# Inverting the softmax sums of a head pair as 16 columns by way of DRAM, in place of a 128x512 reciprocal

## The chip, the cores and the metric

The kernel runs on one core of a Trainium2 chip. The metric is device microseconds of one execution: the median of three runs is 2515.03 us (2510.77 to 2517.75). One more execution was profiled; it took 2517.77 us, and its trace has a span of 2516.0 us.

## The reference, cut to what matters

The program is two transformer blocks over 1024 tokens of width 1024, in float32. Its first block has two attention layers. Layer 0 mixes eight heads of global attention, eight of windowed attention and four memory heads; layer 1 mixes sixteen heads of neighbourhood attention and four memory heads. The part that the change touches is the division in the softmax of the global and the neighbourhood heads:

```
s = jnp.einsum('bqkgd,bskd->bkgqs', qblk, k).astype(jnp.float32) * scale
p = jax.nn.softmax(s, axis=-1).astype(v.dtype)
return jnp.einsum('bkgqs,bskd->bqkgd', p, v)
...
y = jnp.concatenate([ya, yb, ym], axis=-1) * jax.nn.silu(gate)
x = x + y @ w_out_even[e]
```

A sum belongs to a query and a head, so a pair of heads has 2 x 1024 different sums. The second block (a pooling mixer and a convolutional feed-forward part) isn't touched.

## The kernel before, in words

Every matmul operand is split into a high and a low part, and a product is three matmuls (`mm3`, L251 to L255; a weight's low part is `wlo`, made in `sub`, L142). Two streams of work are interleaved. The *attention stream* runs the heads two at a time (`pipe`): `glob_main` for four pairs of layer 0, `win_main` for four windowed pairs, and `nbr_main` for eight pairs of layer 1. The *fill stream* runs the projections (`dense`), which load weights into three buffers `wraw`. `weave` mixes both streams by a planned cost for each step; `ahead` gives the attention stream a higher priority; the framework's scheduler then fixes one order of instructions for each engine ahead of the run. Each engine works through its order strictly, and an instruction that waits holds up what is behind it. All DMAs are issued by SyncE (SP) in one such order (`dma`, L162).

The global and the neighbourhood pairs use `wide`. Their queries lie along 1024 columns in two halves g of 512. O is one buffer of 128 x 1024 (two heads of 64 rows; `bufs` is 1, so the next pair writes it only when this one's is stored). For each head s and key tile, ScalarE computes p, GpSimd (POOL) adds p to `acc[s, g]` (L586), and TensorE adds to o. When a half is complete, `close` copies half of o on ScalarE (`oe`, L605) and VectorE adds the two parts into O (L606). After the second head's half, TensorE sums `acc` over its partitions by matmuls with a matrix of twos: d is a PSUM tile of 128 x 512 in which rows 0 to 63 all hold one head's sums and rows 64 to 127 the other's. VectorE inverts all of d (L618), and POOL multiplies O by the result R (L619). d lies in the one PSUM buffer `r`, which the row-maximum transposes of `max_row` (L461) use too. At the pair's end `finish_pair` loads the gate sg, `back` multiplies O by it on VectorE (L622), and O goes to DRAM (`y<-O`); the last pair of each layer is split into hh and hl instead. `oe`, sg and R share two buffers (tag `oe`); the sums `acc` have four (tag `acc`).

The memory heads (`mem_main`) have a 128x512 reciprocal of their own (L734), which stays.

Of the kernel before, what the change touches and what calls it, by code (L numbers as in the profile page):

```python
# [8 lines left out]
F32 = mybir.dt.float32  # L9
F32R = mybir.dt.float32r  # L10
AF = mybir.ActivationFunctionType
ALU = mybir.AluOpType
# [3 lines left out]
S = 1024  # L16
# [120 lines left out]
def raw(ap):  # L137
    return ap.bitcast(F32) if ap.dtype == F32R else ap


def sub(out_eng, out, a, b):
    out_eng.tensor_tensor(out=out, in0=a, in1=b, op=ALU.subtract)  # L142


class Build:
# [411 lines left out]
    def wide(self, O, U, V, tiles, perm=False):  # L557


        nc = self.nc  # L560
        mm = nc.tensor.matmul
        parts = [[(g, max(a, 512 * g), min(b, 512 * g + 512)) for g in range(2) if max(a, 512 * g) < min(b, 512 * g + 512)] for _, a, b in tiles]
        touch = {g: [i for i, ps in enumerate(parts) if g in [p[0] for p in ps]] for g in range(2)}
        acc, bank = {}, {}

        def sums(s, g):
            acc[s, g] = t = self.po.tile([128, 512], F32, tag="acc", name="acc", bufs=self.accb)
            return t

        def dest(s, i):  # L570

            g, a, b = parts[i][0]
            if (s, g) not in acc:
                return sums(s, g)
            return self.pp.tile([128, b - a], F32, tag="p", name="p", bufs=3)

        def take(s, i, p):

            a = tiles[i][1]
            for g, x0, x1 in parts[i]:  # L580
                if (s, g) not in acc:
                    nc.gpsimd.memset(sums(s, g), 0.0)
                t = acc[s, g]
                if t is not p:
                    t = t[:, x0 - 512 * g:x1 - 512 * g]
                    nc.gpsimd.tensor_tensor(out=t, in0=t, in1=p[:, x0 - a:x1 - a], op=ALU.add)  # L586

        def pv(s, i, P):
            j, a, b = tiles[i]
            for g, x0, x1 in parts[i]:  # L590
                new = (s, g) not in bank
                if new:
                    bank[s, g] = self.op.tile([128, 512], F32, tag="od"[g], name="o")
                o = bank[s, g][:, x0 - 512 * g:x1 - 512 * g]
                x = slice(x0 - a, x1 - a)
                mm(o, V[s][:, j, 2:130], P[0][:, x], start=new, stop=False, skip_group_check=True)
                mm(o[0:64], V[s][:, j, 2:66], P[1][:, x], start=False, stop=i == touch[g][-1], skip_group_check=True)  # L597
                if i == touch[g][-1]:
                    close(s, g)

        def close(s, g):

            o = bank[s, g]
            e = self.po.tile([64, 512], F32, tag="oe", name="oe", bufs=2)
            nc.scalar.copy(e, o[64:128])  # L605
            nc.vector.tensor_tensor(out=self.halfo(O[64 * s:64 * s + 64], g, perm), in0=self.seq(o[0:64], perm), in1=self.seq(e, perm), op=ALU.add)  # L606
            if s == 0:
                return
            d = self.rq.tile([128, 512], F32, tag="r", name="d")
            for i in range(2):  # L610
                h = self.pp.tile([128, 512], F32R, tag="ph", name="ah")
                nc.scalar.copy(h, acc[i, g])
                l = self.pp.tile([128, 512], F32R, tag="pl", name="al")
                sub(nc.gpsimd, l, acc[i, g], raw(h))
                mm(d, self.sel[i], h, start=i == 0, stop=False)
                mm(d, self.sel[i], l, start=False, stop=i == 1)
            R = self.po.tile([128, 512], F32, tag="oe", name="R", bufs=2)
            nc.vector.reciprocal(R, d)  # L618
            nc.gpsimd.tensor_tensor(out=self.halfo(O, g, perm), in0=self.halfo(O, g, perm), in1=self.seq(R, perm), op=ALU.mult)  # L619

        def back(g, sg):
            nc.vector.tensor_tensor(out=self.halfo(O, g, perm), in0=self.halfo(O, g, perm), in1=self.seq(sg, perm), op=ALU.mult)  # L622
        return dest, take, pv, back

    def narrow(self, O, U, V, tiles, groups, sink):
# [28 lines left out]
        def close(s, g, ts):  # L654
# [5 lines left out]
            nc.vector.tensor_tensor(out=e[:, :, 0], in0=e[:, :, 0], in1=sink[s][:, q], op=ALU.add)  # L660
            R = self.small.tile([128, 8], F32, tag="R", name="R")
            nc.vector.reciprocal(R[:, 0:n], e[:, :, 0])
            nc.gpsimd.tensor_tensor(out=T[:, q, s], in0=e[:, :, 2:66], in1=e[:, :, 66:130], op=ALU.add)
            nc.gpsimd.tensor_tensor(out=T[:, q, s], in0=T[:, q, s], in1=R[:, 0:n].unsqueeze(2).to_broadcast([128, n, 64]), op=ALU.mult)

# [992 lines left out]
```

## Time and profile before

| What | us |
|---|---|
| median of three runs | 2515.03 (2510.77 to 2517.75) |
| profiled execution | 2517.77 |
| its span | 2516.0 |
| TensorE (PE) busy | 2397.2, 95% |
| VectorE (DVE) busy | 1809.1, 72% |
| ScalarE (ACT) busy | 1071.7, 43% |
| GpSimd (POOL) busy | 989.7, 39% |
| DMA queue, share of 16 engines | 41.0% |

The global pairs run from about 190 to 560 us of the span and the neighbourhood pairs from about 960 to 1500. A row of the waits names the engine and what it waited for, then the total us, the number of times and the longest one. A busy PE is not PE at its peak, so its granted clock stands beside it. The line numbers are those of the kernel before.

### The profile page before, as it was taken

To read this page: it belongs to the slowest core of one execution; us is meant where nothing else is said; L and a number is where in the kernel's file an instruction comes from. 1 tells how busy PE (TensorE), PEld (TensorE's weight loads), DVE (VectorE), ACT (ScalarE), POOL (GpSimd) and SP (SyncE) were. 2 spreads that over 40 slices of the span, in tenths; PEclk is the share of its full clock that TensorE was granted. 3 is DMA by queue.
4 is the path that set the end of the run, shared out by engine and by line. 5 is a ranking of instruction groups with operands and counts; after the bars stand their busy time and mean duration, and the time that the engine had idled before them with its cause. 6 is when DMAs were issued, how large, how long until landed. Compare 5 with 4: busy or idle time off the path is not lost. (4 is left out here: it accounts for less than half of the span.)

```text
span 2516.0 us, 33273 instructions
## 1 busy us (share of the span) xinstructions
PE 2397.2 (95%) x11320; PEld 1962.2 (78%) x11320; DVE 1809.1 (72%) x2897; ACT 1071.7 (43%) x1873; POOL 989.7 (39%) x833
## 2 busy tenths in 40 slices
PE   7999999999999999999999999998789999999999
PEld 6967777777878788888888877776668888888887
DVE  6778877787787557767888789798967464655554
ACT  5526555554442535444343553444544132323231
POOL 3128886873331226656575762575700000000000
PEclk9999999999899999999999999997979999999999
DMA  6752342344456567766675564321213111111112
GB/s 204 214 135 71 114 109 93 93 128 118 128 186 214 183 190 188 192 191 171 196 204 171 164 238 159 124 82 51 69 45 97 51 49 49 46 51 47 50 47 88
DMA packets 234241, 314.37 MB, mean 125 GB/s; under 512 B 101879, under 2 KB 120823, under 8 KB 234072
## 3 DMA queue, kind: packets, MB, share of 16 engines
q1 hardware_dynamic: 234072, 312.26, 41.0%
q8 instruction: 89, 1.46, 0.2%
q14 instruction: 80, 0.66, 0.1%
HBM read 225.02 MB, written 87.03 MB: 124 GB/s over the span
## 5 line engine op out<-in xcount | busy, mean ns | idle before, releaser
L254 PE MATMUL ps<-hl,whi 128*128 128x512 f32 x1888 | 753.0, 399 | 13.3 <-DVE hl L396 7.8
L251 PE MATMUL ps<-hh,whi 128*128 128x512 f32 x1888 | 749.8, 400 | 15.5 <-ACT hh L395 8.2
L255 PE MATMUL ps<-hh,wlo 128*128 128x512 f32 x1888 | 752.6, 399 | 9.0 <-DVE wlo L142 8.8
L242 ACT CAST whi<-wraw 128x512 fp32r<-128x512 f32 (+1 forms) x416 | 250.7, 606 | 494.9 <-PE ps L254 409.5
L251 PEld LDWEIGHTS ps<-hh,whi 128*128 128x128 f32 x1888 | 363.2, 193 | 92.9 <-ACT hh L395 8.2
L254 PEld LDWEIGHTS ps<-hl,whi 128*128 128x128 f32 x1888 | 363.4, 192 | 92.5 <-DVE hl L396 9.9
L255 PEld LDWEIGHTS ps<-hh,wlo 128*128 128x128 f32 x1888 | 362.8, 192 | 86.1 <-DVE wlo L142 10.8
L586 POOL TENSOR_TENSOR acc<-acc,p 128x512 f32<-128x512 f32 (+2 forms) x272 | 320.0, 1183 | 237.8 <-ACT p L449 186.0
L142 DVE TENSOR_TENSOR wlo<-wraw,whi 128x512 fp32r<-128x512 f32 (+1 forms) x404 | 330.1, 821 | 61.9 <-ACT whi L242 54.3
L142 POOL TENSOR_TENSOR pl<-p,ph 128x512 fp32r<-128x512 f32 (+2 forms) x208 | 259.7, 1251 | 189.4 <-ACT ph L451 163.8
L451 ACT CAST ph<-p 128x512 fp32r<-128x512 f32 (+2 forms) x336 | 181.8, 551 | 40.7 <-PE o L649 10.4
L449 ACT ACTIVATE p<-p 128x256 f32<-128x256 f32 (+2 forms) x192 | 97.7, 515 | 151.0 <-DVE p L1236 94.7
L1480 DVE TENSOR_TENSOR xacc<-ps,xacc 128x512 f32<-128x512 f32 x96 | 66.2, 691 | 131.4 <-PE ps L255 131.0
L1452 DVE TENSOR_TENSOR hz<-ps,rbc 128x512 f32<-128x512 f32 x88 | 60.5, 690 | 116.4 <-PE ps L255 114.2
L142 DVE TENSOR_TENSOR pl<-p,ph 128x512 fp32r<-128x512 f32 (+2 forms) x128 | 115.2, 900 | 39.7 <-ACT ph L451 32.9
L254 PE MATMUL ps<-al,whi 128*128 128x512 f32 x352 | 139.1, 396 | 0.0
L255 PE MATMUL ps<-ah,wlo 128*128 128x512 f32 x352 | 138.8, 396 | 0.0
L251 PE MATMUL ps<-ah,whi 128*128 128x512 f32 x352 | 138.5, 396 | 0.0
L449 ACT ACTIVATE p<-s 128x512 f32<-128x512 f32 x144 | 84.6, 597 | 119.6 <-PE s L538 69.6
L1456 ACT ACTIVATE cv<-hz,vecs 128x512 f32<-128x512 f32 x88 | 71.5, 815 | 130.6 <-DVE hz L1452 125.0
L597 PE MATMUL o<-pl,V 128*64 128x384 f32 (+2 forms) x288 | 94.5, 347 | 3.2 <-DVE pl L142 2.4
L1236 DVE TENSOR_TENSOR p<-s,MB 128x384 f32<-128x384 f32 (+2 forms) x128 | 68.5, 548 | 39.8 <-POOL pl L142 22.5
(268 smaller groups left out, 4563.3 us busy)
## 6 DMA issues: line engine op xcount, KB each, us to landing
wraw<-in_w SPq DMA_DIRECT2D x116, 256.0 KB
wraw<-in_wfi SPq DMA_DIRECT2D x112, 256.0 KB
wraw<-in_wo SPq DMA_DIRECT2D x72, 256.0 KB
g<-evf SPq DMA_DIRECT2D x48, 256.0 KB
wraw<-in_wfo SPq DMA_DIRECT2D x40, 256.0 KB
sg<-g SPq DMA_DIRECT2D x32, 256.0 KB
y<-O SPq DMA_DIRECT2D x14, 512.0 KB
hl<-y SPq DMA_DIRECT2D x14, 512.0 KB
```

Of the source, the lines that this page charges most:

```text
L142: out_eng.tensor_tensor(out=out, in0=a, in1=b, op=ALU.subtract)
L242: nc.scalar.copy(hi, raw[:, q:q + e])
L251: i = mm(ps, wh, h, start=first, stop=False, skip_group_check=True)
L254: mm(ps, wh, l, start=False, stop=False, skip_group_check=True)
L255: mm(ps, wl, h, start=False, stop=last, skip_group_check=True)
L449: nc.scalar.activation(p, s, AF.Exp)
L451: nc.scalar.copy(ph, p)
L586: nc.gpsimd.tensor_tensor(out=t, in0=t, in1=p[:, x0 - a:x1 - a], op=ALU.add)
L597: mm(o[0:64], V[s][:, j, 2:66], P[1][:, x], start=False, stop=i == touch[g][-1], skip_group_check=True)
L1236: nc.vector.tensor_tensor(out=p, in0=ps, in1=MB[:, s, o:o + b - a], op=ALU.add)
L1456: nc.scalar.activation(t, z[:, 2:514], AF.Identity, scale=self.v("cw2", j), bias=self.v("cb", j))
L1480: nc.vector.tensor_tensor(out=x, in0=ps, in1=x, op=ALU.add)
```

## The change

The whole-tile reciprocal and the multiplication directly behind it go. Each half of d is copied by ScalarE as rows 0 to 64, and rows 0 and 64, one for each head, are written to a DRAM tile `dd` of 2 x 1024. After the second half `invert` loads `dd` as 128 partitions x 16 columns, inverts that on VectorE, writes it to a second DRAM tile `dr`, and loads R of both halves by four DMAs that repeat a row over 64 partitions. R now takes buffers of the tag `acc`. POOL's multiplication of O by R moves into `back`, in front of the multiplication by the gate.

```diff
@@ wide @@
         acc, bank = {}, {}
+        dd, dr = [self.dram(n, [2, S], F32) for n in ("dd", "dr")]
+        R = []
...
                 mm(d, self.sel[i], h, start=i == 0, stop=False)
                 mm(d, self.sel[i], l, start=False, stop=i == 1)
-            R = self.po.tile([128, 512], F32, tag="oe", name="R", bufs=2)
-            nc.vector.reciprocal(R, d)
-            nc.gpsimd.tensor_tensor(out=self.halfo(O, g, perm), in0=self.halfo(O, g, perm), in1=self.seq(R, perm), op=ALU.mult)
+            e = self.po.tile([65, 512], F32, tag="oe", name="de", bufs=2)
+            nc.scalar.copy(e, d[0:65])
+            for i in range(2):
+                self.dma(out=dd[i, 512 * g:512 * g + 512], in_=e[64 * i:64 * i + 1])
+            if g == 1:
+                invert()
+
+        def invert():
+
+            c = self.small.tile([128, 16], F32, tag="dc", name="dc")
+            self.dma(out=c, in_=dd.rearrange("h (a b) -> (h a) b", b=16))
+            r = self.small.tile([128, 16], F32, tag="dr", name="dr")
+            nc.vector.reciprocal(r, c)
+            self.dma(out=dr.rearrange("h (a b) -> (h a) b", b=16), in_=r)
+            for g in range(2):
+                R.append(self.po.tile([128, 512], F32, tag="acc", name="R", bufs=self.accb))
+                for i in range(2):
+                    self.dma(out=R[g][64 * i:64 * i + 64], in_=dr[i:i + 1, 512 * g:512 * g + 512].to_broadcast([64, 512]))
 
         def back(g, sg):
+            nc.gpsimd.tensor_tensor(out=self.halfo(O, g, perm), in0=self.halfo(O, g, perm), in1=self.seq(R[g], perm), op=ALU.mult)
             nc.vector.tensor_tensor(out=self.halfo(O, g, perm), in0=self.halfo(O, g, perm), in1=self.seq(sg, perm), op=ALU.mult)
```

## Rows read from the trace of the kernel before

**Rows 1.** Windows: start:end, length, busy us of PE, PEld, DVE, ACT, POOL, PEclk, DMA share, GB/s

```profile
190.00:560.00 370.00, 353.39 (x1544) 273.11 (x1542) 296.77 (x395) 213.08 (x376) 299.75 (x208) 0.98 0.33 101
960.00:1500.00 540.00, 529.04 (x2766) 449.44 (x2765) 419.20 (x694) 244.11 (x475) 337.22 (x324) 0.99 0.65 188
374.00:383.00 9.00, 5.36 (x14) 2.38 (x13) 9.00 (x12) 1.20 (x3) 5.54 (x5) 0.73 0.21 73
1146.00:1154.00 8.00, 5.37 (x18) 3.54 (x17) 8.00 (x18) 1.33 (x3) 1.52 (x1) 0.72 0.59 165
```

**Rows 2.** Groups by line and shape: count, busy us, mean ns, idle before

```profile
L618 DVE RECIPROCAL R<-d 128x512 f32<-128x512 f32 x24 | 80.4, 3350 | 1.4 <-PE d L616 1.3
L619 POOL TENSOR_TENSOR O<-O,R 128x512 f32<-128x512 f32 x24 | 39.7, 1652 | 53.3 <-DVE R L618 51.8 <-DVE negm L1213 1.5
L622 DVE TENSOR_TENSOR O<-O,sg 128x512 f32<-128x512 f32 x24 | 28.1, 1170 | 5.9 <-DMA sg<-g 5.9
L605 ACT COPY oe<-o 64x512 f32<-64x512 f32 x48 | 27.8, 580 | 11.9 <-PE o L597 11.3
...
L359 DVE RECIPROCAL r<-rs 128x16 f32<-128x16 f32 x5 | 1.2, 246 | 1.4 <-ACT rs L357 1.4
```

**Rows 3.** PE's waits in 374:383, 469:473, 1012:1016 and 1147:1152

```profile
PE s L461 <- DVE R L618: 1.4, 1, 1.4
PE o L597 <- DVE pl L142: 1.1, 1, 1.1
PE s L846 <- DVE mcg L847: 0.9, 1, 0.9
...
PE s L461 <- DVE R L618: 1.2, 1, 1.2
PE o L597 <- DVE pl L142: 0.9, 1, 0.9
...
PE ps L251 <- DVE evl L1285: 1.2, 1, 1.2
...
PE ps L255 <- DVE wlo L142: 1.7, 1, 1.7
PE s L461 <- DVE R L618: 0.7, 1, 0.7
```

**Rows 4.** VectorE in order of time: start us, us, line, operation, tiles

```profile
1006.98 3.36 DVE L618 RECIPROCAL R<-d 128x512 f32<-128x512 f32 x1
1010.26 0.39 DVE L1285 SCALAR_TENSOR_TENSOR evl<-ps,rc,evh 128x256 fp32r<-128x256 f32 x1
...
282.73 3.34 DVE L618 RECIPROCAL R<-d 128x512 f32<-128x512 f32 x1
...
299.71 0.67 DVE L606 TENSOR_TENSOR O<-o,oe 64x512 f32<-64x512 f32 x1
...
1435.00 3.35 DVE L618 RECIPROCAL R<-d 128x512 f32<-128x512 f32 x1
...
1449.83 1.06 DVE L606 TENSOR_TENSOR O<-o,oe 64x512 f32<-64x512 f32 x1
```

**Rows 5.** SP's DMA issues in order of time

```profile
1168.20 0.38 SPq L162 DMA_DIRECT2D qc4h<-evh  x1
1169.20 0.33 SPq L162 DMA_DIRECT2D qc4l<-evl  x1
1171.50 1.15 SPq L162 DMA_DIRECT2D U<-qc4h  x2
...
1446.09 0.32 SPq L162 DMA_DIRECT2D y<-O  x1
```

**Rows 6.** Waits of SP and POOL over the span: total us, times, longest

```profile
SPq L162 <- DVE wlo L142: 752.7, 274, 16.1
...
SPq L162 <- DMA x<-xr: 27.4, 10, 4.1
...
POOL O L619 <- DVE R L618: 51.8, 12, 10.6
```

## The prediction, made before the changed kernel was run

> **What bounds the kernel now.** I read the windows by stage first, then the groups by line, then PE's waits, then the order of time on VectorE and SP around a few reciprocals. The windows show that TensorE is the engine that sets the time where the change acts: it is busy 353.4 of 370 us while the global pairs run and 529.0 of 540 us while the neighbourhood pairs do [rows 1]. The reader should see that VectorE's 80.4 us of reciprocals [rows 2] aren't 80 us of the span. What can be had is PE's idle time there, (370 - 353.4) + (540 - 529.0) = 27.6 us, and what a lower clock costs behind a pause. PE's waits show which part of that follows a reciprocal. Eight waits lie in short stretches directly behind four of the 24: three times `max_row`'s matmul waits until R has been read out of the one PSUM buffer `r`, and five times PE waits for something that VectorE had queued behind a reciprocal [rows 3]; one of these is the split of the V projection, which starts at 1010.26, as the 3.36 us reciprocal of 1006.98 ends [rows 4]. Behind two of the four the granted clock has a mean of 0.73 and 0.72, so part of the stretch ran at 1.2 in place of 2.4 GHz [rows 1].
>
> **What goes.** 24 reciprocals of 3.35 us leave VectorE [rows 2]. On the path they are worth what PE waits for them: 1.4 + 1.1 + 0.9 + 1.2 + 0.9 + 1.2 + 1.7 + 0.7 = 9.1 us [rows 3]. The clock adds at most (1 - 0.73) x 9 + (1 - 0.72) x 8 = 4.6 us [rows 1]. Together that is 13.7 us, or 13.7 / 80.4 = 0.17 us of span for each us that VectorE stands in the way; I use this rate below. What is late next in those places is the ScalarE copy of d (0.6 us in place of 3.35), so `r` comes free at least 2.7 us sooner than it does now, more than the longest of the three waits for it (1.4).
>
> **What is added beside other work.** 24 copies of 65 x 512 on ScalarE: the nearest row is the 64 x 512 copy out of PSUM at 0.58 us [rows 2], so 13.9 us. ScalarE is busy 213 of 370 and 244 of 540 us [rows 1], which hides them; if that cover failed everywhere they would cost 13.9 us. Twelve reciprocals of 128 x 16 at 0.25 us [rows 2] are 3 us of VectorE, at the rate 0.5 us; I leave them inside the rounding. The multiplications of O by R are the same 24 at 1.65 us, moved. SP gets ten more DMAs a pair (four writes of `dd`, one load, one write of `dr`, four broadcasts); at the 0.33 to 0.58 us of an issue [rows 5] (the two issues of U take 1.15) that is 3 to 6 us a pair. SP has 752.7 us in which it only waits for a weight buffer [rows 6]; these hide it.
>
> **What is added in series.** Four DMAs now depend on each other: `dd` out, `dd` in, `dr` out, R in. The trace of before has no transfer of 64 bytes a partition and no such chain. The nearest rows are a store and the load of the same tile: the store of qc4h is issued at 1168.20 and its load could be issued at 1171.50, 3.3 us later [rows 5]. On the other side SP stood 27.4 / 10 = 2.7 us, on average, for the store of x1 before it loaded that again [rows 6]. These transfers are 256 KB and the new ones 2 to 128 KB, so a hop may be below 2.7 as well; one that shares the queue with weights, as in the second stage at 188 GB/s [rows 1], may be above 3.3. I take 3.0, between the two rows. R then comes 0.6 (copy) + 4 x 3.0 + 0.25 + 1.0 (three issues behind a first one) = 13.8 us after the point at which the last reciprocal of a pair starts now, and it came 3.35 us after it: 10.5 us later.
>
> Sentences that the sum can do without: the Trainium skill, page "DMA: Bandwidth & Descriptors", section "Anatomy of one DMA — SWDGE (gpsimd) path", gives a small transfer about 2.0 us of fixed cost, nearly all of it the receipt of the write; it measured that on GpSimd's path, and these DMAs are SP's. The rows are above it (2.7 and 3.3), with larger transfers in them. As an estimate by the page, R would come after 0.6 + 8.0 + 0.25 + 1.0 = 9.9 us; the O term below would then be 1.1 in place of 3.7 us, and the sum 2504.5.
>
> **Who waits for R.** First POOL: the multiplication stands in POOL's order, with next pair's `acc` additions and half of its `pl` behind it. POOL stands for R already, 51.8 us in 12 places [rows 6], and no row of PE's waits in the four stretches names POOL [rows 3]. The bounds are 0 and 12 x 10.5 = 126 us of standing, at the rate 0 to 21 us. I take a tenth, 12.6 us or 2.1 us of span, because the order is fixed by a plan that knows of the DMAs, and the standing of today costs nothing visible.
>
> Second, O, which has one buffer. From the old start of the last reciprocal to O's release is now 13.8 + 1.65 + 1.65 (POOL, two halves) + 1.17 (gate, VectorE) + 3.7 (the store: issued at 1446.09, the next write of O follows without idling at 1449.83) = 22.0 us [rows 2, 4, 5]. The next pair's first write of O comes 299.71 - 282.73 = 17.0 us after that start in the first of the ten places where another such pair follows, and 1449.83 - 1435.00 = 14.8 in the last [rows 4]; of the other eight, read in the same way, two are at 15.7 and 18.8 and six at 22 or more. So four writes are late, by 5.0, 6.3, 3.2 and 7.2 = 21.7 us. If VectorE stands for all of that, it costs 21.7 x 0.17 = 3.7 us; 0 if the plan puts other work first, and about 10 if hops are 4.5 us and six of the ten are late. I take 3.7. R in the `acc` buffers meets the next pair's second head only, half a pair later, about 25 us with pairs 60 to 90 us apart; I cost it at nothing.
>
> **The sum.** -13.7 + 3.7 + 2.1 = -7.9 us. The profiled execution takes 2517.8 us, 2.7 above the median of 2515.0; it would become 2509.9, and the median **2507**. About 0.3% (7.5 us) is what a measurement of this kernel can tell from no change, so this stands at that edge.
>
> **The rivals.**
> - *More comes free* (0.12). VectorE is busy 297 of 370 us in the first stage [rows 1]; with 27 us less there, waits go that don't lie behind a reciprocal. At most all 27.6 us of idle time go: 2487; in the middle 2497. Against it: in the second stage PE has only 11 us to give.
> - *Nothing comes of it* (0.18). The fixed order of every engine is planned anew, so other waits of 1 to 2 us open where the eight close, and POOL's and O's terms use up the rest: 2513, within 4.
> - *The chain gets stuck in SP's order* (0.27), and the kernel is slower. SP issues in order and stands 752.7 / 274 = 2.7 us on average before a weight load, 16.1 at the longest [rows 6]. If such a load is ahead of each of the four hops, R is later by another 10.8 us a pair, and POOL stands all of it at the multiplication: 12 x 10.8 = 130 us, at the rate 22 us. The sum is -13.7 + 3.7 + 22 = +12: 2527. It decides from (13.7 - 3.7) / 0.17 = 59 us of POOL's standing, 5 us a pair. For it: an order that waits is SP's normal state. Against it: most of those waits end where the plan expected them, and POOL's standing has not reached PE so far.
>
> The forecast has 0.43, of which 0.31 is faster by over 0.3% and 0.12 within it; its own range is 2500 to 2513. With the rivals: **faster** 0.31 + 0.12 = 0.43; **same** 0.12 + 0.18 = 0.30; **slower** 0.27. The range that should hold the time 8 times in 10 is 2492 to 2529: it takes in the upper part of the first rival's span and the slower rival's 2527.
>
> **What would show it.** Right: no PE wait names R at L461's line; VectorE's busy time is about 77 us less in sum, PE's waits on VectorE in the two stages some 9 us less; SP shows waits for `dd`, `dr` and the small reciprocal of 2 to 4 us each; R lands 11 to 17 us after the last d; the clock stays near 1.0 behind the places that are at 0.72 now. Wrong: POOL waits for R of over 59 us in total with PE waits on `pl` behind them; VectorE waiting for `y<-O` at its write of O for more than 22 us; weights late on ScalarE because SP stood in the chain; or PE's idle time in the two stages at 27 us as before, with other names.

## The result and the profile after

The changed kernel takes 2558.15 us (median of four runs, 2552.0 to 2559.3) where the kernel before takes 2512.9 beside it: a ratio of 1.0173 (95% interval 1.0149 to 1.0198). It is slower, and above the upper end of the range that was given.

I look first for the place of the loss. Four marks exist in both kernels: the row maxima of the global pairs, those of the windowed pairs, those of the neighbourhood pairs, and `hz` of the feed-forward part. The view groups the instructions of one source line; its columns are durations in ns (min/median/max), then the starts of the first and the last one. Before:

```profile
L846 PE MATMUL s<-KA,U x128: 388/396/796, 140.2 to 448.4; 128*128 128x512 f32 x128
...
L909 PE MATMUL s<-KA,U x64: 277/357/689, 466.1 to 666.1; 128*128 128x384 f32 x48, 128*128 128x256 f32 x16
...
L1209 PE MATMUL s<-KB,U x128: 281/332/436, 927.8 to 1410.5; 112*128 112x368 f32 x96, 112*128 112x256 f32 x32
...
L1452 DVE TENSOR_TENSOR hz<-ps,rbc x88: 676/692/693, 1738.1 to 2467.7; 128x512 f32<-128x512 f32 x88
```

The same lines after (they stand 18 lines further down in the code):

```profile
L864 PE MATMUL s<-KA,U x128: 387/397/796, 140.5 to 466.0; 128*128 128x512 f32 x128
...
L927 PE MATMUL s<-KA,U x64: 278/388/667, 484.3 to 693.8; 128*128 128x384 f32 x48, 128*128 128x256 f32 x16
...
L1227 PE MATMUL s<-KB,U x128: 282/332/508, 956.4 to 1442.1; 112*128 112x368 f32 x96, 112*128 112x256 f32 x32
...
L1470 DVE TENSOR_TENSOR hz<-ps,rbc x88: 676/691/692, 1779.7 to 2509.1; 128x512 f32<-128x512 f32 x88
```

Both kernels reach the global pairs at 140 us. By the first neighbourhood matmul the changed one is 956.4 - 927.8 = 28.6 us late; between there and the first `hz` it takes 823.3 in place of 810.3, another 13.0; the feed-forward part takes 729.4 in place of 729.6. So about two thirds of the loss lie in layer 0, one third in layer 1, and none behind the change.

The windows of the two stages after, with the columns of [rows 1]:

```profile
190.00:590.00 400.00, 365.47 (x1537) 279.43 (x1536) 280.01 (x392) 217.46 (x383) 293.95 (x204) 0.94 0.32 98
988.00:1530.00 542.00, 527.28 (x2752) 443.44 (x2750) 376.29 (x675) 250.17 (x482) 335.26 (x322) 1.00 0.66 188
```

The window of the global stage is taken 30 us longer, because the stage's last O add lies at 577.58 in place of 545.41. PE idles 34.5 us in it (400 - 365.5), against 16.6 in [rows 1], and its busy time grows by 12.1 us for the same work (1537 recorded matmuls and 1544) while the mean granted clock falls from 0.98 to 0.94. So of the 30 us about 18 are idle time and 12 a slower PE. In the second stage VectorE is busy 43 us less, and PE has nothing from it: it idles 14.7 us there, against 11.0.

The groups of the changed steps, with the columns of [rows 2]:

```profile
L640 DVE TENSOR_TENSOR O<-O,sg 128x512 f32<-128x512 f32 x24 | 40.4, 1682 | 30.1 <-POOL O L639 30.1
...
L639 POOL TENSOR_TENSOR O<-O,R 128x512 f32<-128x512 f32 x24 | 39.7, 1660 | 128.9 <-DMA R<-dr 128.9
...
L607 ACT COPY oe<-o 64x512 f32<-64x512 f32 x48 | 27.9, 581 | 19.7 <-PE o L599 19.1
...
L620 ACT COPY de<-d 65x512 f32<-65x512 f32 x24 | 13.9, 580 | 17.9 <-PE d L618 17.7
...
L631 DVE RECIPROCAL dr<-dc 128x16 f32<-128x16 f32 x12 | 3.0, 251 | 14.3 <-DMA dc<-dd 14.3
```

The copies and the small reciprocals cost on their engines what was forecast, 13.9 and 3.0 us. The number to stop at is 128.9: POOL stands that long for R, where it stood 51.8 us for the reciprocal [rows 6]. In the view of waits it is twelve places, 18.1 us at the longest:

```profile
POOL O L639 <- DMA R<-dr: 128.9, 12, 18.1
```

PE waits longer for `pl`, half of which POOL makes. Over the span, before and after:

```profile
PE o L597 <- POOL pl L142: 0.6, 1, 0.6
...
PE o L599 <- POOL pl L142: 9.4, 7, 2.7
```

SP waits 727.2 us for weights against 752.7 [rows 6], and `de`, `dd` and `dr` add 71.4 us in 40 places, 1.8 us each on average.

```profile
SPq L162 <- DVE wlo L142: 727.2, 260, 16.6
...
SPq L162 <- ACT de L620: 34.1, 15, 9.3
...
SPq L162 <- DMA dd<-de: 13.0, 6, 3.0
SPq L162 <- DMA dr<-dr: 12.4, 11, 1.9
SPq L162 <- DVE dr L631: 11.9, 8, 2.4
```

Is the way through DRAM longer than thought? The timeline (start, us) of the first pair, put together from ScalarE, SP, VectorE and POOL:

```profile
277.06 0.58 ACT L620 COPY de<-d 65x512 f32<-65x512 f32 x1 [2.91 <-PE d L618]
...
277.67 0.54 SPq L162 DMA_DIRECT2D dd<-de  x2
...
279.87 0.35 SPq L162 DMA_DIRECT2D dc<-dd  x1
...
282.13 0.25 DVE L631 RECIPROCAL dr<-dc 128x16 f32<-128x16 f32 x1
...
282.65 0.42 SPq L162 DMA_DIRECT2D dr<-dr  x1
...
285.98 1.13 SPq L162 DMA_DIRECT2D R<-dr  x2
...
289.74 1.26 POOL L639 TENSOR_TENSOR O<-O,R 128x512 f32<-128x512 f32 x1 [18.10 <-DMA R<-dr]
290.96 1.26 POOL L142 TENSOR_TENSOR pl<-p,ph 128x512 fp32r<-128x512 f32 x1
```

From the copy to the multiplication it is 12.7 us; the prediction had 13.8 to R. Its hops are 2.2, 2.3, 3.3 and 3.8 us, around the 3.0 taken. The odd thing is in POOL's wait: it is 18.1 us, longer than the whole chain. POOL came there at 271.6, and no work of the next pair stands in front of the multiplication; a `pl` of it stands right behind. The next pair should have given POOL sums to add. So I look at when the next pair starts. Its first exponential that goes straight into a new `acc` tile, on ScalarE, and the last O add of the first pair, on VectorE, before:

```profile
266.50 0.61 ACT L449 ACTIVATE acc<-s 128x512 f32<-128x512 f32 x1
...
277.07 0.68 DVE L606 TENSOR_TENSOR O<-o,oe 64x512 f32<-64x512 f32 x1
```

and after:

```profile
283.24 0.58 ACT L449 ACTIVATE acc<-s 128x512 f32<-128x512 f32 x1
...
273.60 0.68 DVE L608 TENSOR_TENSOR O<-o,oe 64x512 f32<-64x512 f32 x1
```

Before, the next pair starts 10.6 us ahead of it, and two pairs overlap; after, it starts 9.6 us behind it. The next two pairs show the same: 8.2 and 8.1 us ahead before, 5.0 and 4.3 behind after. The overlap of the pairs is gone, and R has taken two of the four `acc` buffers.

### The profile page after: what moved, and what is told of

It reads as the page before. It is cut to its first block, busy times and chain, and to the rows that moved or that the text cites. A ratio compares the mean times of both kernels' runs of the same rounds, so it can differ in the third digit from the quotient of the medians.

```text
span 2557.5 us, 33453 instructions
## 1 busy us (share of the span) xinstructions
PE 2409.6 (94%) x11320; PEld 1966.9 (77%) x11320; DVE 1757.6 (69%) x2885; ACT 1086.3 (42%) x1897; POOL 986.9 (39%) x833
## 5 line engine op out<-in xcount | busy, mean ns | idle before, releaser
L251 PE MATMUL ps<-hh,whi 128*128 128x512 f32 x1888 | 750.6, 401 | 23.1 <-ACT hh L395 7.9
L251 PEld LDWEIGHTS ps<-hh,whi 128*128 128x128 f32 x1888 | 364.3, 193 | 101.9 <-ACT hh L395 7.9
L451 ACT CAST ph<-p 128x512 fp32r<-128x512 f32 (+2 forms) x336 | 182.1, 551 | 47.6 <-PE o L667 10.5
L142 DVE TENSOR_TENSOR pl<-p,ph 128x512 fp32r<-128x512 f32 (+2 forms) x128 | 128.3, 1002 | 41.5 <-ACT ph L451 29.2
L251 PE MATMUL ps<-ah,whi 128*128 128x512 f32 x352 | 138.4, 396 | 0.0
L599 PE MATMUL o<-pl,V 128*64 128x384 f32 (+1 forms) x288 | 95.1, 351 | 16.8 <-POOL pl L142 9.4
```

The lines of the kernel that those rows point to most:

```text
L251: i = mm(ps, wh, h, start=first, stop=False, skip_group_check=True)
L451: nc.scalar.copy(ph, p)
```

## The experiments

Each ratio is to the kernel before, run beside it on the same chip. "Layer 0" is the time to the first neighbourhood matmul, "layer 1" from there to the first `hz`, "rest" from there to the last `hz`, in the profiled execution. Layer 0 of seven of these kernels (R0, L7, K0, G1, G2, G3, G4) has the same source and took 921.9 to 928.8, so I don't read a single difference under 7 us in these columns. The rest has the same source in all kernels but H4, H3 and H5, and took 720.3 to 732.1.

| | kernel | median | ratio (interval) | layer 0 | layer 1 | rest |
|---|---|---|---|---|---|---|
| | before, profiled | 2512.9 | 1 | 927.8 | 810.3 | 729.6 |
| | after | 2558.15 | 1.0173 (1.0149–1.0198) | 956.4 | 823.3 | 729.4 |
| NI | no inversion | 2507.38 | 0.9977 (0.9963–0.9991) | 924.8 | 800.7 | 729.8 |
| MV | only moved | 2517.31 | 1.0009 (0.9999–1.0020) | 939.9 | 804.1 | 726.4 |
| RO | R in `oe` | 2531.92 | 1.0067 (1.0052–1.0082) | 930.2 | 824.5 | 729.5 |
| R0 | R out of `acc` in layer 0 | 2524.99 | 1.0038 (1.0022–1.0054) | 926.4 | 824.9 | 724.9 |
| CU | chain unused | 2511.64 | 0.9995 (0.9979–1.0011) | 922.7 | 812.8 | 720.3 |
| L7 | R0, last pair direct | 2523.12 | 1.0039 (1.0023–1.0056) | 925.1 | 818.5 | 726.9 |
| A7 | after, last pair direct | 2549.29 | 1.0146 (1.0129–1.0162) | 956.9 | 821.3 | 721.8 |
| K0 | chain in layer 0 alone | 2503.74 | 0.9965 (0.9952–0.9979) | 921.9 | 808.7 | 720.3 |
| G1 | K0, two ph and pl | 2537.35 | 1.0077 (1.0048–1.0106) | 928.8 | 835.4 | 720.9 |
| G2 | R0, R with own buffers, two ph and pl | 2524.86 | 1.0025 (1.0010–1.0039) | 925.2 | 829.1 | 720.7 |
| G3 | R0, last four pairs direct | 2519.21 | 1.0012 (0.9994–1.0030) | 926.2 | 810.5 | 732.1 |
| G4 | R0, VectorE multiplies in layer 1 | 2537.37 | 1.0080 (1.0053–1.0106) | 925.6 | 833.9 | 725.8 |
| H4 | K0, two wraw | 2556.29 | 1.0152 (1.0126–1.0178) | 941.5 | 827.8 | 737.0 |
| H3 | R0, R with one own buffer, two wraw | 2561.25 | 1.0171 (1.0141–1.0201) | 948.3 | 831.8 | 733.9 |
| H5 | R0, R half in `acc`, two wraw | 2556.49 | 1.0157 (1.0132–1.0182) | 940.5 | 831.3 | 733.1 |

**What are the reciprocals worth?** NI is the kernel before with a copy in place of the inversion.

```diff
-            nc.vector.reciprocal(R, d)
+            nc.scalar.copy(R, d)
```

> The kernel before with each 128x512 reciprocal replaced by a ScalarE copy of d to R; the inversion is left out, all else is as before. It shows what the reciprocals are worth on the path. By my sum (13.7 us for 80.4 us of VectorE) it is 10 to 16 us faster than before. If VectorE's reciprocals were hidden anyway it is within 4 us; if VectorE bounds the two stages it is 25 us faster or more.

It gains 0.23%, some 5.8 us (2.3 to 9.3), and not the 10 to 16 that my sum gave. The term of 13.7 us was too large, by its middle more than twice. This is about what an inversion that takes a ScalarE copy (0.59 us) in place of 3.35 us on VectorE, and no detour, is worth. The row of NI for 190 to 560 us, with the columns of [rows 1], shows where the rest went:

```profile
190.00:560.00 370.00, 353.51 (x1545) 275.48 (x1544) 285.04 (x397) 216.63 (x385) 299.23 (x209) 0.98 0.33 101
```

VectorE is busy 11.7 us less there, and PE is as busy as in [rows 1] (353.4). PE's waits for R are gone; those for the row maxima `mcg` on VectorE are 7.1 us in four places, against 1.5 in two before.

**Is it the move, without the chain?** MV keeps the reciprocals, but gives R the `acc` buffers and multiplies in `back`.

```diff
-            R = self.po.tile([128, 512], F32, tag="oe", name="R", bufs=2)
-            nc.vector.reciprocal(R, d)
-            nc.gpsimd.tensor_tensor(... in1=self.seq(R, perm), op=ALU.mult)
+            R.append(self.po.tile([128, 512], F32, tag="acc", name="R", bufs=self.accb))
+            nc.vector.reciprocal(R[g], d)
...
         def back(g, sg):
+            nc.gpsimd.tensor_tensor(... in1=self.seq(R[g], perm), op=ALU.mult)
```

> The kernel before, its reciprocals kept and no DMA added; only R is moved into the buffers of the sums (tag acc) and POOL's multiplication by R into back, as in the changed kernel. Theory A (R takes the buffers of the sums with which the next pair would start, so two pairs no longer overlap): slower than before by 8 to 25 us although no DMA is in the way. Rival B (POOL stands at the multiplication until the four DMAs are through): within 4 us of before, since R is there 3.4 us after d. Rival C (the added DMAs and SP's order): within 4 us.

In total there is no change (2.3 us by the ratio): theory A's 8 to 25 us are missed, and the total lies where rivals B and C had it. Layer 0 is 12.1 us late all the same, and the first exponentials of the next pairs are 14 to 22 us later than before (280.37, 378.58 and 478.29 against 266.50, 362.12 and 456.06). So R in `acc` alone ends the overlap, but it costs layer 0 less than half of the 28.6 us of the changed kernel. Layer 1 and the rest took 6.2 and 3.2 us less in this execution, differences under the 7 us above, and the total hides the loss.

**R out of `acc`.** RO puts R into `oe` and the gate of `finish_pair` into `acc`. R0 puts R of layer 0 into the 128 x 1024 buffer `sg` that the windowed pairs and the memory heads use, and leaves layer 1 as in the changed kernel.

```diff
# RO
-                R.append(self.po.tile([128, 512], F32, tag="acc", name="R", bufs=self.accb))
+                R.append(self.po.tile([128, 512], F32, tag="oe", name="R", bufs=2))
...
-            sg = self.po.tile([128, 512], F32, tag="oe", name="sg", bufs=2)
+            sg = self.po.tile([128, 512], F32, tag="acc", name="sg", bufs=self.accb)
# R0
+            R2 = None if perm else self.po.tile([128, S], F32, tag="sg", name="R")
-                R.append(self.po.tile([128, 512], F32, tag="acc", ...))
+                R.append(self.po.tile([128, 512], F32, tag="acc", ...) if perm else R2[:, 512 * g:512 * g + 512])
```

> The changed kernel with two tags swapped: R in the buffers oe, the gate sg in the buffers acc (its loads wait for no chain). The chain of DMAs and the place of the multiplication stay. Theory A: the next pair starts early again, the 28 us lost by the end of layer 0 go, and the kernel is at 2500 to 2530 us. Rivals B and C: the chain is as long as before and the kernel stays at 2545 to 2560.

> The changed kernel with R in a buffer that the global pairs don't use otherwise (tag sg) in layer 0 alone; layer 1 as changed. Theory A: the shift at the end of layer 0 goes from 28 us to within 6, the 13 us that layer 1 loses stay: 2525 to 2538 us in all. Rivals B and C: 2550 to 2560.

Both get layer 0 back whole: 930.2 and 926.4 against 927.8 before and 956.4 after. In R0 the next pair starts where it did before; ScalarE:

```profile
266.28 0.59 ACT L449 ACTIVATE acc<-s 128x512 f32<-128x512 f32 x1
```

and POOL, in R0, with its waits in brackets:

```profile
275.67 4.48 POOL L588 TENSOR_TENSOR acc<-acc,p 128x512 f32<-128x512 f32 x3 [1.83 <-DVE pl L142]
280.10 2.98 POOL L142 TENSOR_TENSOR pl<-p,ph 128x512 fp32r<-128x512 f32 x2
...
294.01 1.28 POOL L640 TENSOR_TENSOR O<-O,R 128x512 f32<-128x512 f32 x1 [4.58 <-DMA R<-dr]
```

The chain is the same and R comes no sooner (294.01 against 289.74), but POOL now has the next pair's work in front of the multiplication and stands 4.6 us in place of 18.1. The loss of layer 0 comes from the buffer together with the chain: R in `acc` without the chain is 12.1 us late (MV), the chain with R elsewhere is not late (R0), both together are 28.6 us late. R0 also takes the total from 1.0173 to 1.0038, some 34 of the 43 us. The totals of RO and R0 lie at the edge of what theory A gave (1.9 us above 2530, and at 2525) and far from the rivals' 2545 and more. Layer 1's loss, 14.6 us in R0, stays in both kernels: RO moved R from one tag that the next pair needs to another.

**Do the transfers cost anything by themselves?** CU keeps the reciprocals and adds the whole chain beside them; its four broadcasts end in a DRAM tile that nothing reads.

```diff
             nc.vector.reciprocal(R, d)
+            e = self.po.tile([65, 512], F32, tag="oe", name="de", bufs=2)
+            nc.scalar.copy(e, d[0:65])
+            for i in range(2):
+                self.dma(out=dd[i, 512 * g:512 * g + 512], in_=e[64 * i:64 * i + 1])
+            if g == 1:
+                invert()      # R2 in DRAM
```

> The kernel before, its reciprocals kept, with the whole way through DRAM added beside them: the copy out of PSUM, the stores, the gathered load, the small reciprocal and the four broadcasts, these into a DRAM tile that nothing reads. Theory (the transfers and SP's issues cost next to nothing by themselves; what cost was the buffer and the wait): 2513 to 2520 us. Rival (the transfers, or the added places in SP's, ScalarE's and VectorE's orders, cost the time): 2530 us and above.

No change (0.9995). 24 copies, 12 small reciprocals and ten DMAs a pair cost nothing that can be measured; the broadcasts end in DRAM here, so their writes into R's buffers are not part of it. What costs is to wait for their result in a buffer that others need.

**Is layer 1's loss in the last pair?** Its chain is stretched by SP's and VectorE's orders; SP, VectorE and POOL, after:

```profile
1521.64 1.40 SPq L162 DMA_DIRECT2D dd<-de  x2
...
1533.16 0.53 SPq L162 DMA_DIRECT2D dc<-dd  x1
...
1546.18 0.24 DVE L631 RECIPROCAL dr<-dc 128x16 f32<-128x16 f32 x1
...
1557.23 3.15 SPq L162 DMA_DIRECT2D R<-dr  x4
...
1564.84 2.36 POOL L639 TENSOR_TENSOR O<-O,R 128x512 f32<-128x512 f32 x1
```

That is 43 us from `dd` to the last multiplication, and then PE waits 6.4 us once for the `hh` made from O (`PE ps L251 <- ACT hh L486`). L7 (from R0) and A7 (from the changed kernel) invert the last neighbourhood pair as before.

```diff
-... partial(self.wide, perm=True), bias)
+... partial(self.wide, perm=True, chain=i != 7), bias)
```

> The kernel with R of layer 0 out of the acc buffers (2524.99 us), and the last neighbourhood pair alone inverts its sums by the two 128x512 reciprocals as before, without the way through DRAM. What stands of layer 1's loss in that kernel is 14.6 us between the first neighbourhood s matmul and the FFN's first hz (824.9 against 810.3 us). Theory (the last pair's chain, spread out in SP's and VectorE's order, holds hh[7] and the projection behind it): 10 to 14 of the 14.6 go, 2511 to 2516 us, and PE waits for hh no more at L251. Rival (the multiply by R, at which GpSimd stands in each of the eight pairs, costs it): less than 4 go, 2521 to 2526 us.

> The changed kernel (R in the acc buffers in both layers), with the last neighbourhood pair alone by the two 128x512 reciprocals. Theory (two causes that add: 28.6 us in layer 0 from R in acc, 13.0 in layer 1 from the last pair's chain): the first neighbourhood s matmul stays 26 to 31 us late and the total is 2544 to 2550 us. Rival (layer 1's loss lies in the pairs before): 2554 to 2560 us.

The two don't agree: A7 gains 0.27%, and its total is in the theory's range, L7 nothing (1.0039 against 1.0038), as the rival had it, although the long chain and the wait for `hh` are gone from both. In the profiled executions A7 has only 2.0 us of its gain in layer 1 and 7.6 in the rest, which no edit touches; L7's layer 1 is 6.4 us shorter. The intervals of the steps overlap, so I can only say that the last pair holds between none and 9 us, and that the wait that looked worst does not carry layer 1's loss.

**The chain in layer 0 alone.** K0 is R0 with `chain=False` for all eight neighbourhood pairs.

> The way through DRAM in the four global pairs of layer 0 alone, R in a 128x1024 buffer of tag sg, the eight neighbourhood pairs with their reciprocals as before. Theory: layer 0 ends 1 to 2 us ahead of before, layer 1 takes its 810 us, so 2508 to 2514 us, and the way through DRAM is worth no more than a third of the 6 us that the kernel without inversions shows. Rival (the eight reciprocals of layer 0 are worth more than their share once no buffer holds the next pair): 2503 to 2507 us.

K0 beats both kernels: 2503.74 us, ratio 0.9965. It met the rival's range. POOL waits for R 8.8 us there in all four pairs. In the profiled executions 5.9 of its 16.7 us come from layer 0 and 9.3 from the feed-forward part, which no edit touches, so I don't claim that the eight reciprocals are worth 9 us.

**Buffer, multiplying engine or chain in layer 1?** G2 gives R of layer 1 two buffers of its own, 4 KB a partition. They are paid for with one buffer each of the tags ph and pl, 2 KB each (three become two in layer 1); G1 is the control that pays the same, but has the reciprocals in layer 1. G3 uses the chain in the first four neighbourhood pairs. G4 lets VectorE multiply by R in layer 1.

```diff
# G1 and G2
-        ph = self.pp.tile([128, n], F32R, tag="ph", name="ph")
+        ph = self.pp.tile([128, n], F32R, tag="ph", name="ph", bufs=self.phb)   # 2 in layer 1; pl, ah, al alike
# G2
-... tag="acc", name="R", bufs=self.accb) if perm else ...
+... tag="R", name="R", bufs=2) if perm else ...
# G3
+... partial(self.wide, perm=True, chain=i < 4), bias)
# G4
-            nc.gpsimd.tensor_tensor(... in1=self.seq(R[g], perm), op=ALU.mult)
+            (nc.vector if perm else nc.gpsimd).tensor_tensor(... in1=self.seq(R[g], perm), op=ALU.mult)
```

> A control for the next kernel: the kernel with the way through DRAM in layer 0 alone (2503.74 us), with two buffers in place of three for each of the split halves of the exponentials (tags ph and pl) in layer 1, which frees 4 KB a partition there. No theory of the chain speaks of it: 2500 to 2520 us, by how much VectorE and TensorE miss the third buffer.

> The way through DRAM in all twelve pairs, R outside the acc buffers in both layers: in layer 0 in the sg buffer, in layer 1 in two buffers of its own, paid for by the two ph and pl buffers of the control. Theory A (in layer 1 too it is R in the acc buffers that sets GpSimd's multiply ahead of the next pair's sums, and the next pair stands; 14 us): at most 5 us above the control. Rival B (the chain itself, its transfers and the wait of O, costs the 14 us in layer 1 whatever buffer R has): 10 to 20 us above the control.

> R of layer 0 in the sg buffer; in layer 1 the first four pairs go through DRAM with R in acc, the last four keep the reciprocals. In the kernel with the last pair alone direct, the last O add of the fourth neighbourhood pair stands 12 us ahead of the same pair of the layer-0-only kernel (267.3 against 279.3 us after the first s matmul), that of the eighth 14 us behind (560.3 against 546.4). Theory (the stand of GpSimd costs only in the last four pairs): 2498 to 2506 us. Rival (the lead is borrowed from the projections beside it and is given back): 2508 to 2516 us.

> The kernel with R of layer 0 in sg (2524.99 us), where in layer 1 VectorE in place of GpSimd multiplies O by R, just ahead of its multiply by the gate. Theory A1 (GpSimd standing at the multiply with the next pair's adds behind it costs layer 1's 14 us): 2511 to 2518 us. Rival A2 (the next pair's sums wait for R's buffers, whoever multiplies): 2522 to 2530 us; rival A3 (VectorE now stands in its place, with the biases of the next pair behind it): 2530 us and above.

The control is slow by itself, 17 us above its expected range. Beside it G2 is 12.5 us faster, with intervals that don't meet; in the profiled executions the difference is 9.9 us, and 6.3 of it lie in layer 1. Rival B, by which the chain costs layer 1 10 to 20 us whatever buffer R has, is out where the control's payment is made. Whether it is out without the payment isn't shown: no kernel has R in `acc` and the payment, and a layer that is late by the payment may have cover for other waits. G3 met neither range: its median is the one of before (2519.21 against 2519.07 beside it), 0.47% above K0's. It has layer 1's time back in the profile (810.5 against 808.7 in K0), so the lead of the first four pairs is given back, as its rival said. Most of what stands between G3 and K0 in the profiled executions is in the rest (732.1 against 720.3), which has the same source in both.

G4 shows best that the buffer is waited for. Its time lies in A3's range and 7 us above A2's, but VectorE waits for R only 15.9 us in 7 places in the whole run. In the neighbourhood pairs (1200 to 1520) the waits of POOL in G4 read:

```profile
POOL acc L588 <- ACT p L449: 54.9, 12, 14.8
POOL acc L584 <- DVE O L640: 53.0, 5, 20.6
```

L584 clears a new `acc` tile of the next pair, and L640 is the multiplication by R. POOL doesn't touch R any more, and it stands 53.0 us all the same, until somebody else has used R up and the buffer comes free. That is A2's wait, the held buffer. The kernel before and K0 have no such row. What this wait costs of the span G4 doesn't show, since its time is not the one that A2 gave. In L7 the other form is seen, where POOL itself multiplies:

```profile
1278.36 0.98 POOL L584 MEMSET acc<- 128x512 f32 x2
1279.32 0.74 POOL L588 TENSOR_TENSOR acc<-acc,p 128x256 f32<-128x256 f32 x1
1292.69 1.55 POOL L646 TENSOR_TENSOR O<-O,R 128x512 f32<-128x512 f32 x1 [12.63 <-DMA R<-dr]
...
1295.15 2.37 POOL L646 TENSOR_TENSOR O<-O,R 128x512 f32<-128x512 f32 x1
1297.49 1.18 POOL L588 TENSOR_TENSOR acc<-acc,p 128x256 f32<-128x256 f32 x1
1298.61 0.52 POOL L584 MEMSET acc<- 128x512 f32 x1
```

Two `acc` tiles of the next pair are cleared, then the multiplication stands 12.6 us, and the third tile is cleared only behind it.

**A cheaper payment?** H4, H3 and H5 pay with one of the three staging buffers for weights (2 KB a partition). H4 is the control, H3 gives R of layer 1 one buffer that both halves share, H5 puts half of R into it and half into `acc`.

```diff
-            raw = self.wp.tile([128, m], F32, tag="wraw", name="wraw", bufs=self.wp.bufs - 1)
+            raw = self.wp.tile([128, m], F32, tag="wraw", name="wraw", bufs=self.wp.bufs - 2)
# H3
+... tag="R", name="R", bufs=1) if perm else ...
# H5
+... tag=("R", "acc")[g], name="R", bufs=(1, self.accb)[g]) if perm else ...
```

> A control for the next two kernels: the kernel with the way through DRAM in layer 0 alone (2503.74 us) with two in place of three staging buffers for weights (tag wraw), which frees 2 KB a partition. No theory of the chain speaks of it: 2500 to 2520 us, by how much the weights' prefetch misses the third buffer.

> The way through DRAM in all twelve pairs; R of layer 0 in the sg buffer, R of layer 1 in a single 128x512 buffer of its own, which both halves use one after the other, paid for by the control's staging buffer. Theory A (R in acc costs layer 1's 14 us): at most 6 us above the control, the second half's load behind the first half's multiply being some 4 us of a wait that nothing stands behind. Rival B (the chain costs it whatever buffer R has): 10 to 20 us above the control.

> As the one before, but R of layer 1's first half in the buffer of its own and that of the second half in an acc buffer. Theory A (a next pair needs all four acc buffers, so one held sets the multiply ahead of its sums as two do): 8 to 16 us above the control. Rival (half the buffers, half the cost): 3 to 8 us. Rival B: as for the one before, 10 to 20 us, in both.

The payment costs far more than the 2500 to 2520 us that were expected: H4 is 1.9% above K0. H3 is 5.0 us above its control, within theory A's 6, but the two intervals overlap; H5 is 0.2 above it, where A had 8 to 16 and every other theory at least 3. With weights late everywhere, a held `acc` buffer seems to have cover; this set decides nothing on layer 1.

## Why the prediction was wrong

**The step that failed** is one sentence: "R in the `acc` buffers meets the next pair's second head only, half a pair later ... I cost it at nothing." It cost the 28.6 us of layer 0, all of which R0 gets back by another buffer for R. Neither part costs that alone: the buffer without the chain makes layer 0 12.1 us late (MV), the chain with another buffer not at all (R0). The price is that of a long wait for a result whose buffer the next pair needs. The sentence asks when the next pair needs R's buffers again, and takes the order of the code for the answer; it doesn't ask how early the next pair starts. Before, the next pair's first sums begin 8 to 11 us ahead of the last O add, and four `acc` buffers are just what such an overlap uses. The two times stood in the trace of before (266.50 and 277.07) and weren't read. Why the fixed order puts the whole next pair behind R, where two of its four buffers are free sooner, no row shows.

**The mis-sized term** is the gain: 13.7 us against 5.8 in NI. The waits of [rows 3] were there, but behind a wait that goes there is another: in NI PE is busy 353.5 of the 370 us, as before, with the waits for `mcg` in place of those for R. The rival "nothing comes of it" described this, and priced it at 2513.

**The chain** was right for most pairs: 12.7 us against 13.8 in the first, with hops of 2.2 to 3.8 against 3.0, and 10.5 to 13.6 from copy to multiplication in nine of the twelve. The Trainium skill, page "DMA: Bandwidth & Descriptors", section "Anatomy of one DMA — SWDGE (gpsimd) path", has about 2.0 us of fixed cost for a small transfer on GpSimd's path. On SP's path a hop can be shorter here: in the second pair the store of `dr` is issued at 387.02 and the load that waits for it at 388.46, 1.4 us later, less than the page's figure. **What was put beside other work** was right as well: CU adds all of it for nothing. No wait of PE names R at L461 any more. VectorE's busy time fell by 51.5 us (1809.1 to 1757.6), not by 77: the multiplications by the gate take 40.4 us in place of the 28.1 in [rows 2], and some 14 us stay unplaced.

**O's term** (3.7 us) didn't come. In the first pair O is stored at 296.93 and next written at 313.16, 16 us later; no wait of VectorE names the store. The late pairs have made room for it: the loss in one place paid for the other.

**POOL's standing** was to grow by 12.6 us and grew by 128.9 - 51.8 = 77.1. The slower rival had 130 us of it and a threshold of 59, and so came nearest, with the right sign, at 2527. The sign of being wrong that the prediction gave for it, over 59 us of standing with waits of PE for `pl` behind it, is there (128.9 us, and 9.4 us of PE's waits for POOL's `pl`). But its reason was mostly wrong: the orders of SP and VectorE made the chain much longer only in the last pair (43.8 us from copy to multiplication), which carries at most a part of layer 1's loss, and somewhat longer in the first and fifth of the neighbourhood pairs (19.1 and 16.1 us). That it came nearest is in this respect luck. And the rate was wrong: at 0.17 us of span for each us of standing, 77.1 us are 13 us; the span grew by 2557.5 - 2516.0 = 41.5. A rate that is read where VectorE is late by 3 us among other work need not hold for an engine that stands with the next pair's work behind it; that is my reading, and no run tests the rate by itself.

**Layer 1's 13 us** are settled in part. Shown: R holds `acc` buffers for which the next pair's sums wait (G4's row), and with buffers of its own the chain does better than the reciprocals by 12.5 us beside the same payment (G2 against G1). Not shown: that this wait is what the 13 us are made of. No kernel with the chain in all of layer 1 got its time back, and H5 missed the range that the held buffer gave it. How the loss is shared among the eight pairs stays open too, and what the chain would be worth there if the memory were free.

## What to carry to other kernels

Before a long wait replaces a short one, ask what its result is kept in, and who takes that buffer next: transfers that cost nothing by themselves (CU) cost a whole overlap when a buffer of the next round is held for their result. Read how far consecutive rounds overlap (the first write of the next against the last of this one) before a tag is shared. And price what is removed by an experiment that leaves it out: here 5.8 us (2.3 to 9.3) would have shown that there was little to win. K0's 0.35% does not contradict this, since the two intervals overlap.

## What the runs showed that I had not expected

The feed-forward part is the same source in every kernel but H4, H3 and H5, and it took 720.3 to 732.1 us. Between the kernel before (729.6) and K0 (720.3) the difference lies in its first 180 us. Windows from the first `hz`, with the length, PE's busy time, clock, DMA share and GB/s, before:

```profile
1738.10:1918.10 180.00, 156.14 (x616) 0.89 0.20 63
```

and in K0:

```profile
1730.60:1910.60 180.00, 159.82 (x657) 0.93 0.22 67
```

K0 gets through 41 more matmuls there at a higher granted clock; the three windows that follow are alike (788 and 790, 786 and 785, 790 and 790 matmuls, all at 1.00). A gain of 0.35% can so come in part from a stage far behind the edit.

Buffers are dear in this kernel: by their ratios, one buffer less of ph and pl in one layer costs 1.1% (G1 against K0), and one weight staging buffer less 1.9% (H4 against K0), several times what the whole change could win.
